# A hybrid decoder step: the first stage in chunk-sized pieces, with logits and two key tiles chunk by chunk

## The chip, the cores and the metric

The kernel runs on one core of one Trainium2 chip. The metric is device time in microseconds (us) from the first to the last instruction of a run with what the runtime adds around it, as the median of several runs. The engines are named as in the profile: PE (TensorE), DVE (VectorE), ACT (ScalarE), POOL (GpSimd) and SP (SyncE, which issues nearly all DMAs here).

## The reference

One trunk layer of a hybrid decoder, for 1024 prompt tokens and 8 sequences of 8 sample tokens (together 1088 columns, d_model 1024):

```python
proj = rmsnorm(h, norm_mix) @ w_in                 # q, k, v, z, b, a, swa q/k/v, merge gates
qkv_c = silu(causal_conv(qkv, conv_buf, conv_w))   # width 4, per channel
q = l2norm(q) * dk**-0.5 ; k = l2norm(k)           # 8 heads of 128
beta = sigmoid(b) ; g = -exp(a_log) * softplus(a + dt_bias)
# gated delta rule in chunks of 64 tokens: cumulative g, decay, a unit lower triangular
# solve of (k*beta) k^T * decay for each chunk and head, then a scan over the chunks
h = h + (sigmoid(gates_a) * o_a + sigmoid(gates_b) * o_b) @ w_out    # o_b: sliding-window attention
h = h + relu(rmsnorm(h, norm_ffn) @ w_up)**2 @ w_down
h = h + sigmoid(rmsnorm(h, norm_ple) @ w_ple_gate) * (p_l @ w_ple_proj)
```

The last factor, `p_l @ w_ple_proj`, depends on nothing else; the kernel computes it first and keeps it in DRAM (`ppd`) until the end.

## The kernel before

Activations stand transposed: 128 features on the partitions, 1088 token columns in the free dimension. The columns are worked in three chunks, `CH`, of 384, 384 and 320. Each fp32 operand of a large product is split into a high part and the rest (`xh`, `xl` for x, `wh`, `wl` for a weight tile), and a product is three matmuls: high by high, low by high, high by low (L166 to L168). One output tile of 128 features is eight k-steps of three matmuls for each of three chunks. A weight tile of 128x1024 is loaded by SP (L119, `wr`, three buffers), split by ACT (L134, `wh`) and POOL (L135, `wl`; the first two on DVE), in the order of the list `order` at L107. Results of PE come in `ps`, three PSUM banks; small ones in `pst`, `psc` (two banks each) and `psn` (one).

The first stage (L274 to L341) does three things side by side:

- p is loaded in three transfers (L284), split on ACT (L286) and DVE (L287), and multiplied into eight output tiles, `ple(f)` (L320). A tile is worked whole: three chunks, evacuated by ACT into one buffer `ppo` of 128x1088 (L328, four buffers), then stored to `ppd` in one DMA of 544 KB (L332).
- x is loaded by chunk in two halves (L294). `x_norm(i)` (L303) squares a chunk on ACT (L306), adds on DVE (L309) and calls `rsqrt_pe` (L238): a matmul with ones (L247, `psn`), scale on DVE (L250), the power -0.5 on POOL (L251), a diagonal `dg` on DVE (L256) and a matmul with it (L257) that lays the factors out along the columns. Then eight times: the scaled x (L316, DVE), `xh` (L317, ACT), `xl` (L318, DVE for two of eight, else POOL).
- The tuple at L335 writes the order of the pieces by hand: `(0, 1, 2, n0, n1, n0, n0, 3, n1, n2, n1, 4, 5, n2, n2, 6, 7)`, a number being one `ple` tile and n0 to n2 the next piece of a chunk's norm.

Each engine then runs its instructions in the order given by a scheduler, which no engine leaves.

After that stage come the logits of the gates (L388, 48 matmuls of 32 rows), their transposes (L427, L430), a chain of some 40 small DVE instructions that makes `beta` and `g` (`gates_tm`, L393 to L422), cumulative sums by matmuls (L435 to L437, L452 to L454), transposes (L465 to L468), and `gcr` stored to DRAM (L469, L473). The key stage follows (L618 to L634): for each of eight heads `conv_steps` (L491) makes one output tile of w_in (order index 8 + h) into `raw` (L500, L502), convolves it (L509 on ACT, L511 three times on DVE, tanh L513, then L522 and L523 into `kT`); `key_rows` (L551) loads the decay row of the head into the one buffer `E` (L556), adds the mask (L558), takes exponents (L564), stores it as `Ed` (L566) and transposes `kT` (L532); `key_products` (L582), one head later, multiplies keys with keys (L591, L592, L593) and stores `kkL` (L596). After heads 3 and 7 the stored products are loaded as `LT` (L601). From there the triangular solve runs on DVE, with L678 and L687 at its head and L666 and L667 as its steps.

## Time and profile of the kernel before

| | |
|---|---|
| Runs (device us) | 2144.75, 2151.54, 2156.72; median 2151.54 |
| The profiled execution | 2145.25 us, its span 2143.5 us |
| Mean granted TensorE clock | 0.989 |
| Busy share | PE 97%, DVE 51%, ACT 37%, POOL 33% |
| Chain that ended last | PE 79%, DVE 10%, ACT 5%, issue 3% |
| DMA | 196.49 MB, mean 92 GB/s |

The profile shows one execution, with all times from the span's start. In the rows further down a line reads: start, duration, engine, line of the kernel, operation, output and inputs, size, count, and in brackets how long the engine was idle just before, with what ended the wait. Matmuls overlap in the rows: what one costs is the distance between two starts. The PEclk of a stretch is the granted clock of TensorE as a share of full speed.

### The profile page before, as it was taken

The numbers are of one execution on the slowest core, as the hardware profiler recorded it, in microseconds if no ns is written. First come the engines' busy times: TensorE is split into PE (matmuls) and PEld (weight loads), VectorE is DVE, ScalarE is ACT, GpSimd is POOL, SyncE is SP. The second block draws the span as 40 slices with busy tenths as digits, with TensorE's granted clock in tenths as the row PEclk, the third lists the DMA queues.
The fourth block names the chain that finished last, engine by engine and source line by source line (L and its number), as shares of the span: only waits on it lengthen the run. The fifth ranks groups of instructions, "written<-read, shape, count | busy, mean of one in ns | idle before, by whom it ended". The sixth has DMA issues, their size and how long they took to land.

```text
span 2143.5 us, 33612 instructions
## 1 busy us (share of the span) xinstructions
PE 2072.6 (97%) x13485; PEld 1994.1 (93%) x13485; DVE 1082.6 (51%) x1717; ACT 798.1 (37%) x1959; POOL 715.1 (33%) x675
## 2 busy tenths in 40 slices
PE   7999999789999999999998999999999999999999
PEld 6899899678889999999998999999999999999998
DVE  6444499787654555455556444233332323333654
ACT  6476434477643443344334223122121212212321
POOL 3332456243235445554456122121212121212121
PEclk9999999899999999999999999999999999999999
DMA  6365343333243223322341221111111111111132
GB/s 238 122 218 182 115 147 109 117 114 119 77 142 103 72 94 121 108 78 71 112 135 64 102 71 44 46 47 43 49 41 50 40 50 40 50 40 50 40 127 80
DMA packets 89063, 196.49 MB, mean 92 GB/s; under 512 B 33612, under 2 KB 44748, under 8 KB 88780
## 3 DMA queue, kind: packets, MB, share of 16 engines
q1 hardware_dynamic: 88908, 194.35, 28.0%
q8 instruction: 106, 1.74, 0.3%
q14 instruction: 49, 0.40, 0.1%
HBM read 145.48 MB, written 50.78 MB: 92 GB/s over the span
## 4 chain that ended last, share of the span: by engine, by line
PE 79%; DVE 10%; ACT 5%; issue 3%; POOL 1%; DMA 1%; SPq 0%; ACTq 0%; DVEq 0%; POOLq 0%
PE ps L166 23%; PE ps L168 22%; PE ps L167 22%; DVE fs L666 2%; DVE LT L667 2%; PE psn L975 1%; PE pst L953 1%; ACT wh L134 1%; DVE nm L938 1%; PE psc L1278 1%; ACT pst L572 1%; ACT pr L940 1%; PE psc L1273 1%; PE pst L1147 1%; PE psc L930 1%
## 5 line engine op out<-in xcount | busy, mean ns | idle before, releaser
L135 POOL TENSOR_TENSOR wl<-wr,wh 128x1024 fp32r<-128x1024 f32 x140 | 342.3, 2445 | 904.6 <-ACT wh L134 904.4
L166 PE MATMUL ps<-xh,wh 128*128 128x384 f32 (+1 forms) x1800 | 624.5, 347 | 3.0 <-ACT qf L350 1.6
L167 PE MATMUL ps<-xl,wh 128*128 128x384 f32 (+1 forms) x1800 | 597.5, 332 | 0.0
L168 PE MATMUL ps<-xh,wl 128*128 128x384 f32 (+1 forms) x1800 | 594.5, 330 | 0.0
L166 PEld LDWEIGHTS ps<-xh,wh 128*128 128x128 f32 x1800 | 341.6, 190 | 14.3 <-issue 9.5
L167 PEld LDWEIGHTS ps<-xl,wh 128*128 128x128 f32 x1800 | 342.3, 190 | 1.3 <-issue 1.1
L134 ACT ACTIVATE wh<-wr 128x1024 fp32r<-128x1024 f32 x143 | 150.8, 1054 | 517.0 <-PE ps L167 441.8
L168 PEld LDWEIGHTS ps<-xh,wl 128*128 128x128 f32 x1800 | 340.6, 189 | 1.6 <-issue 0.7
L166 PE MATMUL ps<-uh,wh 128*128 128x384 f32 (+1 forms) x768 | 250.7, 326 | 1.2 <-DVE h L1429 1.2
L168 PE MATMUL ps<-uh,wl 128*128 128x384 f32 (+1 forms) x768 | 250.9, 327 | 0.0
L167 PE MATMUL ps<-ul,wh 128*128 128x384 f32 (+1 forms) x768 | 250.5, 326 | 0.0
L1429 DVE TENSOR_TENSOR h<-h,ps 128x384 f32<-128x384 f32 (+1 forms) x192 | 100.5, 530 | 226.3 <-PE ps L168 226.3
L166 PE MATMUL ps<-ph,wh 128*128 128x384 f32 (+1 forms) x600 | 196.3, 327 | 0.0
L167 PE MATMUL ps<-pl,wh 128*128 128x384 f32 (+1 forms) x600 | 196.2, 327 | 0.0
L168 PE MATMUL ps<-ph,wl 128*128 128x384 f32 (+1 forms) x600 | 196.0, 327 | 0.0
L1415 DVE TENSOR_TENSOR ul<-us,uh 128x384 fp32r<-128x384 f32 (+1 forms) x96 | 98.0, 1022 | 115.3 <-ACT uh L1414 115.3
L166 PEld LDWEIGHTS ps<-uh,wh 128*128 128x128 f32 x768 | 144.2, 188 | 2.0 <-DVE h L1429 2.0
L168 PEld LDWEIGHTS ps<-uh,wl 128*128 128x128 f32 x768 | 144.2, 188 | 0.0
L167 PEld LDWEIGHTS ps<-ul,wh 128*128 128x128 f32 x768 | 144.1, 188 | 0.0
L511 DVE SCALAR_TENSOR_TENSOR cacc<-raw,cw,cacc 128x1112 f32<-128x1112 f32 x72 | 109.5, 1521 | 59.5 <-ACT cacc L509 58.1
L1413 ACT ACTIVATE us<-ut 128x384 f32<-128x384 f32 (+1 forms) x96 | 48.2, 502 | 196.0 <-DVE ut L1412 194.5
L1412 DVE SCALAR_TENSOR_TENSOR ut<-ps,rb 128x384 f32<-128x384 f32 (+1 forms) x96 | 51.3, 535 | 136.2 <-PE ps L168 136.2
(415 smaller groups left out, 3442.5 us busy)
## 6 DMA issues: line engine op xcount, KB each, us to landing
wr<-win SPq DMA_DIRECT2D x60, 512.0 KB
wr<-wup SPq DMA_DIRECT2D x32, 512.0 KB
wr<-wdn SPq DMA_DIRECT2D x32, 512.0 KB
ppd<-ppo SPq DMA_DIRECT2D x8, 544.0 KB
kTd<-kT SPq DMA_DIRECT2D x8, 544.0 KB
Ed<-E SPq DMA_DIRECT2D x8, 544.0 KB
rg<-Ed SPq DMA_DIRECT2D x8, 544.0 KB
gkT<-kTd SPq DMA_DIRECT2D x8, 544.0 KB
```

The costliest lines, as they stand in the source:

```text
L134: act(hv, rv, AF.Copy)
L135: (nc.gpsimd if i > 1 else nc.vector).tensor_tensor(lv, rv, hv.bitcast(F32), ALU.subtract)
L166: mm(ps[:M, :w], a, h[:, c0 : c0 + w], start=(k == 0), stop=False)
L167: mm(ps[:M, :w], a, l[:, c0 : c0 + w], start=False, stop=False)
L168: mm(ps[:M, :w], b, h[:, c0 : c0 + w], start=False, stop=(k == n - 1))
L511: stt(out=cc, in0=raw[:, j : j + CONVW], scalar=cw[:, f, j : j + 1], in1=cc, op0=ALU.mult, op1=ALU.add)
L666: tt(tmp, X[:, j : j + 1, j + 1 :].broadcast_to(sh), X[:, 0:j, j : j + 1].broadcast_to(sh), ALU.mult)
L667: tt(X[:, 0:j, j + 1 :], X[:, 0:j, j + 1 :], tmp, ALU.add)
L1412: stt(out=t, in0=ps[:, :w], scalar=0.0, in1=rb2[:, c0 : c0 + w], op0=ALU.max, op1=ALU.mult)
L1413: act(s, t, AF.Square)
L1415: tt(lo[:, c0 : c0 + w], s, hi[:, c0 : c0 + w].bitcast(F32), ALU.subtract)
L1429: tt(hc, hc, ps[:, :w], ALU.add)
```

## The change

The order of the first stage is written out anew, in pieces of one chunk:

- The four steps of a projection tile go chunk by chunk: `ple(fs, i)` does the tiles of the list fs for chunk i alone, each into a buffer `ppo` of 128x384 (13 buffers, shared with the pieces of p). Their stores (`spill`) are 24 of 192 or 160 KB instead of 8 of 544 KB, and come later.
- p is loaded in six transfers instead of three, half of x chunk 0 before p chunk 1, the constants before x chunks 1 and 2.
- The squares stand in two half buffers; `rsqrt_steps` yields once more, between the power and the diagonal.
- The narrow weight `wba` (for the logits) moves behind the first key tile in the order of weights, with split buffers of its own.
- The logits and the first two key tiles (order index 8 and 9) are no longer done after all of x is ready, but chunk by chunk between the norms. Their raw results have buffers of their own. Everything that follows them (gate chain, both convolutions) starts when the third chunk of each is done.

```diff
-    order = [(d["wpp"][u], 1024) for u in range(2)] + [(d["wba"], 128)]
+    order = [(d["wpp"][u], 1024) for u in range(2)]
     order += [(d["win"][f], 1024) for f in WIN_ORDER]
+    order.insert(3, (d["wba"], 128))
...
-        for step in (0, 1, 2, n0, n1, n0, n0, 3, n1, n2, n1, 4, 5, n2, n2, 6, 7):
-            if isinstance(step, int):
-                ple(step)
-            else:
-                next(step, None)
...
+    p_chunk(0)
+    w_load()
+    w_split()
+    x_chunk(0, 0)
+    p_chunk(1)
+    x_chunk(0, 4)
+    p_chunk(2)
+    w_load()
+    w_split()
+    load_constants()
...
+    def spill(fs, i):
+        c0, w = CH[i]
+        for f in fs:
+            dma(ppd[f, :, c0 : c0 + w], ppo[f, i][:, :w])
...
+    A, B1, B2 = range(4), range(4, 6), range(6, 8)
+    ple(A, 0)
+    ple(A, 1)
+    next(n0)
+    spill(A, 0)
+    ple(A, 2)
+    next(n0)
+    ple(B1, 0)
+    next(n0)
+    next(n0, None)
+    next(n1)
+    spill(A, 1)
+    spill(A, 2)
+    ple(B1, 1)
+    ple(B1, 2)
+    next(n1)
+    ple(B2, 0)
+    next(n1)
+    next(n1, None)
+    next(n2)
+    ple(B2, 1)
+    ple(B2, 2)
+    dma(cache, d["cachec"])
...
+    first = [conv_steps(8 + h, lambda: kp, key_tile, ep.tile([P, RAWW], F32, name="raw0", tag="tg")) for h in range(2)]
+    logits = logit_steps()
+    next(first[0])
+    next(logits)
+    next(first[1])
+    next(n2)
+    next(n2)
+    next(n2, None)
+    for st in (first[0], logits, first[1]):
+        next(st)
+    for i in range(3):
+        spill(B1, i)
+        spill(B2, i)
+    for st in (logits, *first):
+        next(st)
...
     for h in range(H + 2):
-        st = conv_steps(8 + h, kp, key_tile) if h < H else feature_steps()
-        next(st)
-        if h > 1:
+        if h < 2:
+            st = first[h]
+        else:
+            st = conv_steps(8 + h, kp, key_tile) if h < H else feature_steps()
+            next(st)
             key_products(*todo.pop(0))
-        next(st)
-        next(st)
+            next(st)
+            next(st)
```

The scheduler's order on ACT, in the middle of the first stage, before: `ppo` is the evacuation of a projection bank, `xh` the high part of a scaled column group.

```order
L306 ACTIVATE xsq<-xc_155 128x4x320
L317 ACTIVATE xh<-xc_139 128x384 x2
L306 ACTIVATE xsq<-xc_155 128x4x320
L317 ACTIVATE xh<-xc_139 128x384 x4
L134 ACTIVATE wh<-wr 128x8x16
L317 ACTIVATE xh<-xc_139 128x384
L328 ACTIVATE ppo<-ps 128x384 x2
L317 ACTIVATE xh<-xc_139 128x384
L328 ACTIVATE ppo<-ps 128x320
```

And now, at the same place:

```order
L404 ACTIVATE ppo<-ps 128x384 x3
L384 ACTIVATE xh<-xc_126 128x384
L404 ACTIVATE ppo<-ps 128x384
L384 ACTIVATE xh<-xc_126 128x384 x2
L404 ACTIVATE ppo<-ps 128x320
L137 ACTIVATE wh<-wr 128x1024
L384 ACTIVATE xh<-xc_126 128x384 x4
L404 ACTIVATE ppo<-ps 128x320
L384 ACTIVATE xh<-xc_126 128x384
```

Banks were emptied only after seven `xh`; now evacuations stand between them, but the last one of this place still stands behind the split of a whole weight tile and four `xh`.

On PE before, the gates' products stood in the first key tile (`ps<-xl,wh` and the like), 35 products after its start:

```order
L166 MATMUL ps<-xh,wh 128x384
L435 MATMUL pst<-g,cst 128x64
L436 MATMUL pst<-g,cst 128x64
L437 MATMUL pst<-g,cst 128x64
L452 MATMUL pst<-gs,c_82 64x8
L453 MATMUL pst<-gs,c_82 64x8
L167 MATMUL ps<-xl,wh 128x384
L454 MATMUL pst<-gbs,cst 128x64
L168 MATMUL ps<-xh,wl 128x384
```

And now they stand in the fourth key tile, four products after its start, and the first head's key products (L664, the L591 of before) come ahead of them:

```order
L171 MATMUL ps<-xh,wl 128x384
L664 MATMUL psc<-kT 128x128 x8
L169 MATMUL ps<-xh,wh 128x320
...
L169 MATMUL ps<-xh,wh 128x384
L543 MATMUL pst<-g,cst 128x64
L544 MATMUL pst<-g,cst 128x64
L545 MATMUL pst<-g,cst 128x64
L560 MATMUL pst<-gs,c_82 64x8
L561 MATMUL pst<-gs,c_82 64x8
```

The gates moved from the first key tile to three tiles later, behind a product that needs the first head's finished `kT`.

On DVE before, the gate chain was over when the first convolution came:

```order
L422 SCALAR_TENSOR_TENSOR gs<-lg,ea 64x8
L450 TENSOR_TENSOR gbs<-gs,c_82 64x64
...
L653 TENSOR_TENSOR dec_2461<-dec_2461,msk_2462 64x64
L511 SCALAR_TENSOR_TENSOR cacc<-raw,cw,cacc 128x1112 x2
L558 TENSOR_TENSOR E<-E,cst 128x1024
L511 SCALAR_TENSOR_TENSOR cacc<-raw,cw,cacc 128x1112
L560 TENSOR_TENSOR E<-E,c_82 64x64
L522 SCALAR_TENSOR_TENSOR kT<-raw,cacc 128x1024
```

And now two convolutions (`raw_520` and `raw_521`, lines L315 and L326) stand within the gate chain:

```order
L315 SCALAR_TENSOR_TENSOR cacc<-raw_520,cw,cacc 128x1112
L522 TENSOR_TENSOR lg_864<-lg_864 128x64
L522 TENSOR_TENSOR lg_893<-lg_893 64x8
L315 SCALAR_TENSOR_TENSOR cacc<-raw_521,cw,cacc 128x1112
L523 TENSOR_SCALAR lg_864<-lg_864 128x64
L523 TENSOR_SCALAR lg_893<-lg_893 64x8
L326 SCALAR_TENSOR_TENSOR kT<-raw_520,cacc 128x1024
...
L528 SCALAR_TENSOR_TENSOR lg<-lg_893,lg 64x8
L326 SCALAR_TENSOR_TENSOR kT<-raw_521,cacc 128x1024
L530 SCALAR_TENSOR_TENSOR g<-lg,ea 128x64
```

Before, no convolution stood ahead of `g`; now two whole ones do.

Farther on DVE, the decay row of head 4 (`E<-E,cst`) before, between the convolutions of the last two key tiles:

```order
L511 SCALAR_TENSOR_TENSOR cacc<-raw,cw,cacc 128x1112 x3
L558 TENSOR_TENSOR E<-E,cst 128x1024
L560 TENSOR_TENSOR E<-E,c_82 64x64
L522 SCALAR_TENSOR_TENSOR kT<-raw,cacc 128x1024
L523 SCALAR_TENSOR_TENSOR kT<-raw,cacc 128x64
L592 TENSOR_TENSOR kk<-psc,E 128x512 x2
L511 SCALAR_TENSOR_TENSOR cacc<-raw,cw,cacc 128x1112 x3
```

And now:

```order
L315 SCALAR_TENSOR_TENSOR cacc<-raw,cw,cacc 128x1112 x3
L631 TENSOR_TENSOR E<-E,cst 128x1024
L633 TENSOR_TENSOR E<-E,c_82 64x64
L665 TENSOR_TENSOR kk<-psc,E 128x512 x2
L326 SCALAR_TENSOR_TENSOR kT<-raw,cacc 128x1024
L327 SCALAR_TENSOR_TENSOR kT<-raw,cacc 128x64
L631 TENSOR_TENSOR E<-E,cst 128x1024
```

The convolution ahead of head 4's decay row is now that of the last key tile, and none follows: four heads' rows come behind it one after the other. From the 1122nd row of PE before (the 1128th now) the two programs have the same rows on every engine.

## Rows read from the trace of the kernel before

**Rows 1.** The page: busy time by engine, and the chain that ended last by engine.

```profile
PE 2072.6 (97%) x13485; PEld 1994.1 (93%) x13485; DVE 1082.6 (51%) x1717; ACT 798.1 (37%) x1959; POOL 715.1 (33%) x675
PE 79%; DVE 10%; ACT 5%; issue 3%; POOL 1%; DMA 1%; SPq 0%; ACTq 0%; DVEq 0%; POOLq 0%
```

**Rows 2.** PE, the instructions that ended a wait in the first 100 us; with 69.45 and 73.65 the heads of two groups of the gates' products, with 70.65 and 74.51 the product of the key tile that follows each; 93.39 is the first matmul of the third key tile.

```profile
12.43 0.96 PE L166 MATMUL ps<-phi,wh 128*128 128x320 f32 x2 [1.22 <-ACT phi L286]
33.45 0.69 PE L166 MATMUL ps<-phi,wh 128*128 128x384 f32 x1 [3.33 <-ACT ppo L328]
48.22 0.68 PE L257 MATMUL pst<-dg,cst 128*128 128x128 f32 x4 [3.07 <-DVE dg L256]
69.45 0.41 PE L435 MATMUL pst<-g,cst 128*128 128x64 f32 x2 [1.66 <-DVE lg L420]
70.65 0.69 PE L167 MATMUL ps<-xl,wh 128*128 128x384 f32 x1
73.65 0.41 PE L465 MATMUL pst<-cst,gc 128*64 128x128 f32 x1
74.51 0.69 PE L167 MATMUL ps<-xl,wh 128*128 128x384 f32 x1
93.39 0.42 PE L166 MATMUL ps<-xh,wh 128*128 128x384 f32 x1
```

**Rows 3.** Stretches of the first stage and, last, one of the key stage: the stretch, its length, then busy time (and count) of PE, PEld, DVE, ACT and POOL, the granted clock, the DMA share and GB/s.

```profile
33.40:39.60 6.20, 6.10 (x20) 5.81 (x21) 6.20 (x8) 2.50 (x6) 5.26 (x5) 0.50 0.50 174
39.60:48.20 8.60, 5.55 (x35) 5.21 (x34) 6.35 (x12) 5.08 (x12) 7.35 (x8) 1.00 0.59 206
48.20:53.40 5.20, 5.17 (x22) 4.19 (x23) 4.16 (x11) 2.72 (x6) 1.71 (x2) 0.67 0.01 2
60.60:69.40 8.80, 7.19 (x44) 6.50 (x43) 7.34 (x43) 2.89 (x9) 3.32 (x9) 1.00 0.29 101
69.40:77.20 7.80, 7.75 (x30) 6.49 (x31) 1.57 (x9) 2.25 (x13) 0.00 (x0) 0.56 0.02 4
197.70:204.00 6.30, 6.09 (x44) 5.44 (x45) 0.04 (x1) 5.90 (x24) 1.81 (x2) 1.00 0.93 280
```

**Rows 4.** SP's issues of the first four projection stores.

```profile
18.96 6.54 SPq L332 DMA_DIRECT2D ppd<-ppo  x4
```

**Rows 5.** DVE: beginning, two members and end of the gate chain; one step of the first convolution and the `kT` that ends it.

```profile
62.02 0.29 DVE L401 COPY lg<-pst 128x64 f32<-128x64 f32 x2 [5.44 <-PE pst L430]
62.82 1.83 DVE L406 TENSOR_SCALAR beta<-beta 128x64 f32<-128x64 f32 x1
64.99 0.15 DVE L406 TENSOR_SCALAR betas<-betas 64x8 f32<-64x8 f32 x1
69.60 0.22 DVE L450 TENSOR_TENSOR gbs<-gs,c 64x64 f32<-64x64 f32 x1
87.99 1.37 DVE L511 SCALAR_TENSOR_TENSOR cacc<-raw,cw,cacc 128x1112 f32<-128x1112 f32 x1
90.73 1.22 DVE L522 SCALAR_TENSOR_TENSOR kT<-raw,cacc 128x1024 f32<-128x1024 f32 x1 [1.25 <-ACT raw L513]
```

**Rows 6.** ACT, tanh and first factor of a convolution; POOL, the weight split that ran beside the gate chain.

```profile
89.58 1.11 ACT L513 ACTIVATE raw<-cacc 128x1112 f32<-128x1112 f32 x1
97.20 1.22 ACT L509 ACTIVATE cacc<-raw,cw 128x1112 f32<-128x1112 f32 x1
62.21 2.39 POOL L135 TENSOR_TENSOR wl<-wr,wh 128x1024 fp32r<-128x1024 f32 x1 [0.83 <-ACT wh L134]
```

**Rows 7.** SP, one turn of the decay buffer: head 5's row stored, head 6's loaded.

```profile
197.28 0.33 SPq L566 DMA_DIRECT2D Ed<-E  x1
...
200.32 0.33 SPq L556 DMA_DIRECT2D E<-gcd  x1
```

**Rows 8.** DVE, the decay buffer in the later heads: mask and first product of head 4, the convolution of the last key tile, mask (ended by the landing of the row) and first product of head 6, first product of head 7.

```profile
175.86 1.22 DVE L558 TENSOR_TENSOR E<-E,cst 128x1024 f32<-128x1024 f32 x1
178.50 0.68 DVE L592 TENSOR_TENSOR kk<-psc,E 128x512 f32<-128x512 f32 x1
187.68 5.71 DVE L511 SCALAR_TENSOR_TENSOR cacc<-raw,cw,cacc 128x1112 f32<-128x1112 f32 x3 [7.38 <-ACT cacc L509]
205.04 2.82 DVE L558 TENSOR_TENSOR E<-E,cst 128x1024 f32<-128x1024 f32 x1 [7.30 <-DMA E<-gcd]
209.45 0.69 DVE L592 TENSOR_TENSOR kk<-psc,E 128x512 f32<-128x512 f32 x1 [1.46 <-ACT E L564]
225.14 0.69 DVE L592 TENSOR_TENSOR kk<-psc,E 128x512 f32<-128x512 f32 x1 [1.26 <-ACT E L564]
```

**Rows 9.** The key products on PE: those of heads 0 and 1 from the chain of waits, those of head 6 from the timeline.

```profile
98.25 1.78 PE psc L591 x16
113.39 1.78 PE psc L591 x16
...
197.71 2.18 PE L591 MATMUL psc<-kT 128*128 128x128 f32 x16 [1.66 <-ACT kb L593]
```

**Rows 10.** The head of the solve: SP's load of the last four heads' products, and DVE's first instructions of the solve.

```profile
230.05 0.79 SPq L601 DMA_DIRECT2D LT<-kkL  x2
241.61 0.80 DVE L678 TENSOR_TENSOR bsol<-bsol,rk 128x64 f32<-128x64 f32 x1 [14.61 <-ACT rk L677]
242.71 5.46 DVE L687 TENSOR_TENSOR LT<-LT,br 128x1024 f32<-128x1024 f32 x4
```

More of the change, by code (lines that the diff above doesn't have):

```diff
@@ L112, in hybrid_layer @@
     order += [(d["wpg"][f], 1024) for f in range(KT)]
-    wst = dict(raw=[], split=[], used=0)
+    wst = dict(raw=[], split=[], used=0, narrow=None)
     def w_load():
@@ L263, in col_rsqrt_pe @@
         for c0, w in CH:
-            rsqrt_pe(acc[:, c0 : c0 + w], c0, w, mul, add, rb, np_)
+            for _ in rsqrt_steps(acc[:, c0 : c0 + w], c0, w, mul, add, rb, np_):
+                pass
     def squares(src, np_):
@@ new lines, in hybrid_layer, with ple @@
+    wpl, ppo = [None, None], {}
+    def ple(fs, i):
+        c0, w = CH[i]
+        for f in fs:
+            if f % 4 == 0 and i == 0:
+                wpl[:] = next_w()
+            ppo[f, i] = pp.tile([P, 384], F32, name="ppo", tag="ppo", bufs=13)
+            ps = pg.tile([P, 512], F32, name="ps", tag="ps")
+            for k in range(2):
+                o = k * 512 + f % 4 * P
+                wh, wl = (z[:, o : o + P] for z in wpl)
+                h_, l_ = (z[:, c0 : c0 + w] for z in prhs[k])
+                mm(ps[:, :w], wh, h_, start=(k == 0), stop=False)
+                mm(ps[:, :w], wh, l_, start=False, stop=False)
+                mm(ps[:, :w], wl, h_, start=False, stop=(k == 1))
+            act(ppo[f, i][:, :w], ps[:, :w], AF.Copy, scale=0.5)
@@ new lines, in spill @@
+    def spill(fs, i):
+        c0, w = CH[i]
+        for f in fs:
+            dma(ppd[f, :, c0 : c0 + w], ppo[f, i][:, :w])
+    A, B1, B2 = range(4), range(4, 6), range(6, 8)
+    n0, n1, n2 = (x_norm(i) for i in range(3))
+    ple(A, 0)
[16 more added lines that the diff above has]
+    next(n1, None)
@@ new lines, in hybrid_layer, with logit_steps, key_tile @@
+    next(n2)
+    ple(B2, 1)
+    ple(B2, 2)
+    dma(cache, d["cachec"])
+    def logit_steps():
+        wb, _ = next_w()
+        for c0, w in CH:
+            ps = pg.tile([P, 512], F32, name="ps", tag="ps")
+            for k in range(KT):
+                for i in range(2):
+                    mm(ps[:32, :w], wb[:, k * 32 : k * 32 + 32], xs[k][i][:, c0 : c0 + w], start=(k + i == 0), stop=(k + i == KT))
+            act(ba[:, c0 : c0 + w], ps[:32, :w], AF.Copy)
+            yield
+    def key_tile():
+        kT = kp.tile([P, NP + MS], F32, name="kT", tag="kT")
+        nc.gpsimd.memset(kT[:, T:], 0.0)
+        return kT
```

198 lines of the change are left out of this document (89 added, 109 removed).

## The prediction

> **What bounds the kernel now.** I read the page first: PE is busy 97% of the span and carries 79% of the chain that ended last [rows 1]. Nothing here removes a matmul, so a gain can come only from time in which PE waits or runs at a lower clock. Such time lies in the first 94 us. The waits of PE there [rows 2] are 1.22 us for the third piece of p, 3.33 us for a bank that ACT empties late, 3.07 us for the diagonal of chunk 2, and 1.66 us for the gates. The stretches show more [rows 3]: 3.05 us idle between 39.6 and 48.2 (8.60 less 5.55), 1.61 us between 60.6 and 69.4, and after each long wait a granted clock of 0.50, 0.67 and 0.56, the 1.2 GHz level for most of those stretches. What the change is worth is therefore how much earlier the third key tile, at 93.39 [rows 2], can begin, less what is given back before the next thing that sets the end, the start of the solve on DVE at 242.71 [rows 10]. From there the programs are the same, row for row.
>
> **The change, part by part: what it saves.** Seven terms, each as the time by which the third key tile comes earlier.
>
> - Projection chunk by chunk. Four tiles of chunk 0, then of chunk 1, need p's last piece some eight groups later than before. The 1.22 us at 12.43 go: **1.2 us**.
> - The bank wait at 33.45. Evacuations are now spread between the `xh`, but the last bank stands behind a weight split and four more `xh`. I keep the wait and the slow stretch behind it (6.20 us at 0.50): **0**. If both went, it would be 3.33 and half of 6.20, together 6.4 us; that is the upper bound.
> - The wait for chunk 2. PE now has two pieces of key tiles of 24 products and a piece of the logits of 16 to do while chunk 2's factors are made; of 3.05 us idle I keep half: **1.5 us** (bounds 0 and 3.05).
> - The slow stretch behind that wait: 5.20 us at 0.67 would be 3.5 us at full clock: **1.7 us**.
> - The idle 1.61 us between 60.6 and 69.4, gate wait included, leave this place: **1.6 us**.
> - The stretch 69.4 to 77.2, 7.80 us at 0.56, becomes 4.4 us: **3.4 us**.
> - The gates' own products leave: 69.45 to 70.65 and 73.65 to 74.51, 2.06 us at the low clock, so about 1.0 us of the 4.4, and I add 1.0 us for the logits' transposes, which run in the stretch from 60.6: **2.0 us**.
>
> The sum is 1.2 + 1.5 + 1.7 + 1.6 + 3.4 + 2.0 = **11.4 us**; the third key tile starts near 82 instead of 93.4.
>
> Three edits cost nothing. The weight list's new order: the split that it moves runs on ACT and POOL while PE has a piece of the projection to do; the cover gone, it is one 2.39 us of POOL [rows 6]. The half-size squares: the same elements on ACT and DVE. The constants before x chunks 1 and 2: chunk 1's factors are not reached before POOL has finished the `xl` of chunk 0.
>
> The stores are 24 instead of 8, the loads of p six instead of three. The first four issues of 544 KB took 6.54 us on SP, waits included [rows 4]; 16 more stores at a few tenths of a microsecond each are some 6 us of SP, spread over 60 us in which SP feeds no load that PE waits for. I price them at 0; the bound, if a weight load queues behind a whole group of them, is 6.54 us once.
> The Trainium skill, "DMA: Bandwidth & Descriptors", section "Bandwidth", advises batches of at least 1 MiB for 75% of the peak, which speaks against cutting 544 KB into 192 and 160 KB. By it the bound of 6.5 us and not 0 would stand in the sum, and the front would gain 4.9 instead of 11.4 us. The trace agrees only in part: from 33.4 us on, where most of the stores now lie, the first stage moves 2 to 206 GB/s [rows 3], which leaves room for slower transfers.
>
> **What it gives back.** Both convolutions and the gate chain now begin together, when the third chunk of tiles 8 and 9 is evacuated, around 78 to 80 us. A convolution on DVE is three steps of 1.37 us and 1.22 us for `kT` (with the sample columns 1.4), with tanh on ACT (1.11) and the first factor (1.22) [rows 5, 6]; 5.6 us of DVE each. The gate chain ran from 62.02 to 69.82, 7.8 us [rows 5]. DVE has thus 19 us to do from about 79.7, all in front of `g`, which is ready near 98.5.
>
> - PE reaches head 0's key products 48 products into tile 10, about 8.3 us after its start, at 90. `kT` needs four of the convolution steps, about half of the gates and one tanh: 79.7 + 5.5 + 3.9 + 1.1 + 1.4 = 91.6, with the ACT hand-overs near 92. Wait: **2.1 us** (bounds 0, and 5.6 if both convolutions are finished first).
> - PE reaches the gates 28 products farther, near 97.2, and waits to 98.5: **1.3 us** (bounds 0 and 3.4, the gates' wait with a stretch at the low clock).
> - The gates' products and transposes are done here at full clock: **2.0 us**.
>
> Do these waits bring the low clock again? The gates' 1.66 us did, after a stretch in which PE was busy 7.19 of 8.80 us; the 1.66 us at 197.71 did not (clock 1.00) [rows 3, 9]. What precedes now is a stretch without idle time, which is nearer to 197.71, so 0; the bound is 3.4 us.
>
> What remains at head 1 is 11.4 - 2.1 - 1.3 - 2.0 = **6.0 us**. Head by head PE then takes 15.14 us (98.25 to 113.39 [rows 9]) as before.
>
> **The start of the solve.** It needs `rk` (ACT, before 241.61) and the loaded products, issued at 230.05 [rows 10]. The first comes from PE and is 6 us earlier. The second hangs on one buffer, E. Head 4's row now stands on DVE behind the convolution of the last key tile: 187.68 less 6.0, plus 5.71, is 187.4, against 175.86 before [rows 8]. From there heads 4 to 7 follow each other through the one buffer. One turn before: store at 197.28, load at 200.32, mask at 205.04, first product at 209.45 [rows 7, 8]; 12.2 us, or 10.6 if the mask takes 1.22 and not 2.82; with two products of 0.69 ahead of the store 12.0 to 13.6. The last turn took 15.7 (209.45 to 225.14), with other work of DVE in it. Head 7's first product thus comes between 187.4 + 2.6 + 3 x 12.0 = 226.0 and 187.4 + 2.6 + 13.6 + 2 x 15.7 = 235.0, against 225.14. I take 228.5, in the lower half, since only the last turn held such other work; the load is then issued 3.4 us later, at 233.4. A row of 512 KB took 4.7 us from issue to the mask, and this load is twice that size, so it lands 4.7 to 9.4 us after: 238.1 to 242.8. The solve starts there, and not at 242.71 less 6.0. I take the lower end, as both halves are issued at once: 242.7 - 238.1 = 4.6, and **4 us** in round terms is what is left. It is reckoned against the profiled execution: 2145.25 - 4 = 2141.3. That run lies 6.3 us under the median of 2151.54; runs scatter by 12 us. From the middle of the two, 2148.4, I forecast **2144 us**. About 0.5%, 10.7 us, is what a measurement can tell from no change.
>
> **The rivals.**
>
> *The gain is kept, or more* (0.28). The waits at head 0's products and at the gates don't occur since ACT and DVE overlap better, and the bank wait shrinks: 11.4 - 2.0 = 9.4 up to 15.8 us with the 6.4 of the bank. For it: DVE was busy only 1.57 of the 7.80 us from 69.4 [rows 3], so that work put there is cheap. Against it: the order stands, `kT` behind gates and convolution. Time 2132.6 to 2139.
>
> *The gain is swallowed* (0.15): the DVE backlog is longer, and clock and waits come back at the new place. Price 3.4 for the clock, and the difference in the gates: the `beta` of 128x64 took 1.83 us while a weight split of 2.39 us ran on POOL from 62.21, its 64x8 sister 0.15 [rows 5, 6]; three such splits fall into the backlog, each up to 1.7 us more, 5 in all. 4 less 3.4 less up to 5 is -4.4 to +0.6: time 2148 to 2153.
> The Trainium skill, "SBUF — State Buffer", section "Who interferes with whom", states the rule for that: VectorE and GpSimd share a pair of ports under an exclusive lock, and the loser blocks for a whole instruction. By that rule each split costs DVE an instruction's length, the 1.83 us agree with it, and the time would be the upper of the two.
>
> *Slower: the one decay buffer sets the solve* (0.15). The change keeps all gains in front, but head 4 waits for the last tile's convolution. Its point: a solve later than 242.71 needs head 7's first product after 228.4 if the load takes 9.4 us, after 233.1 if it takes 4.7. At 235.0 the load is issued at 239.9 and lands at 244.6 to 249.3, so the solve starts 1.9 to 6.6 us later than before: 2150 to 2155. For it: the convolution ahead of head 4's row is one tile later. Against it: the turn before was bound by other DVE work at the last head.
>
> **How the numbers follow.** Forecast 0.42 (its own range 2140 to 2148), kept 0.28, swallowed 0.15, decay buffer 0.15. Range 2128 to 2156: the kept gain's 2132.6 with most of the runs' half scatter of 6 us below it, and the upper end of the slower cases with 1 us. Faster by over 10.7 us: most of the kept case and a little of the forecast, 0.30. Slower by over 10.7 us: the ends of the two slower cases, 0.07. Within: 0.63.
>
> **What will show it.** Third key tile's first matmul near 82; no wait of 1.2 us at p; the bank wait still there near 33; waits of 2.1 and 1.3 us near 92 and 98; the solve's first use of the products near 239, its releaser the load rather than `rk`. A first tile not earlier than 88, or a solve after 243, makes the prediction wrong.

## The result and the profile after

The changed kernel is **slower**: 2158.13 us as the median of 20 runs, against 2147.23 us for the kernel before (20 runs); the ratio is 1.0045 with a 95% interval of 1.003 to 1.006, some 10 us. The forecast was 2144 us and its range ended at 2156. The profiled execution took 2160.55 us, with a span of 2158.8 us.

The front went nearly as forecast. The stretches of the first stage after, which answer to [rows 3], with the same columns:

```profile
28.00:33.40 5.40, 1.58 (x9) 1.00 (x7) 5.40 (x9) 4.92 (x11) 5.06 (x5) 1.00 0.94 317
33.40:39.60 6.20, 2.68 (x10) 2.31 (x11) 5.18 (x3) 2.45 (x5) 6.20 (x4) 0.51 0.26 87
39.60:48.20 8.60, 8.60 (x44) 8.60 (x45) 5.65 (x11) 4.57 (x9) 1.80 (x5) 0.76 0.71 223
60.60:69.40 8.80, 8.45 (x49) 6.74 (x48) 5.82 (x13) 4.18 (x10) 5.97 (x8) 1.00 0.00 0
69.40:77.20 7.80, 7.80 (x51) 7.17 (x50) 0.00 (x0) 1.32 (x4) 2.28 (x10) 1.00 0.01 2
```

The stretch from 69.4 ran at full clock with 51 matmuls in place of 30 at 0.56. The waits of PE after, from the timeline, with the starts of key tiles among them, each the first product at 128x384 (L169). The third key tile, which is number 10 in the order of weights, starts at 83.31 and answers to 93.39 in [rows 2]; tiles 13, 14 and 15 start at 131.77, 149.26 and 171.71:

```profile
8.01 0.69 PE L401 MATMUL ps<-phi,wh 128*128 128x384 f32 x1 [8.01 <-ACT wh L137]
...
32.20 0.41 PE L401 MATMUL ps<-phi,wh 128*128 128x320 f32 x1 [3.77 <-ACT ppo L404]
...
38.80 1.41 PE L250 MATMUL psn<-cst,xsq 128*128 128x1 f32 x6 [3.51 <-DVE xsq L377]
...
83.31 0.45 PE L169 MATMUL ps<-xh,wh 128*128 128x384 f32 x1
...
93.48 2.05 PE L664 MATMUL psc<-kT 128*128 128x128 f32 x16 [1.57 <-DVE kT L326]
...
131.77 0.34 PE L169 MATMUL ps<-xh,wh 128*128 128x384 f32 x1
...
134.29 2.19 PE L664 MATMUL psc<-kT 128*128 128x128 f32 x16 [1.64 <-ACT kb L666]
...
149.26 0.34 PE L169 MATMUL ps<-xh,wh 128*128 128x384 f32 x1
...
152.11 3.10 PE L664 MATMUL psc<-kT 128*128 128x128 f32 x16 [2.34 <-ACT kb L666]
...
169.77 2.18 PE L664 MATMUL psc<-kT 128*128 128x128 f32 x16 [1.31 <-ACT kb L666]
...
171.71 0.42 PE L169 MATMUL ps<-xh,wh 128*128 128x384 f32 x1
...
236.88 0.69 PE L169 MATMUL ps<-xh,wh 128*128 128x384 f32 x1 [5.34 <-ACT qf L290]
...
242.38 0.48 PE L213 MATMUL psc<-nhi,sel 128*2 128x384 f32 x1 [4.17 <-ACT nhi L222]
```

Tile 10 starts 10.1 us earlier than before, and tile 13 7.1 us (131.77; 138.83 in the timeline of before). Tile 14 is 4.7 us ahead (153.99 before), tile 15 2.6 us behind (169.14 before). Then come waits of 5.34 and 4.17 us; with one of 0.28 us behind them they make 9.8 us, where the kernel before had 3.2 at this place (231.77 to 234.67 in its timeline). The key products of all eight heads, grouped, show the same (durations in ns: least, median, greatest; then the starts of the first and the last); first the changed kernel, then the one before:

```profile
L664 PE MATMUL psc<-kT x128: 271/276/516, 93.5 to 226.1; 128*128 128x128 f32 x128
```

```profile
L591 PE MATMUL psc<-kT x128: 270/275/377, 98.1 to 214.1; 128*128 128x128 f32 x128
```

4.6 us earlier with the first head, 12.0 us later with the last: the lead is lost, and more, between them.

On DVE the decay rows and the head of the solve, which answer to [rows 8] and [rows 10]:

```profile
112.48 1.23 DVE L631 TENSOR_TENSOR E<-E,cst 128x1024 f32<-128x1024 f32 x1 [0.54 <-DMA E<-gcd]
129.55 1.22 DVE L631 TENSOR_TENSOR E<-E,cst 128x1024 f32<-128x1024 f32 x1
147.38 1.22 DVE L631 TENSOR_TENSOR E<-E,cst 128x1024 f32<-128x1024 f32 x1
159.50 5.62 DVE L315 SCALAR_TENSOR_TENSOR cacc<-raw,cw,cacc 128x1112 f32<-128x1112 f32 x3 [7.36 <-ACT cacc L313]
165.03 1.22 DVE L631 TENSOR_TENSOR E<-E,cst 128x1024 f32<-128x1024 f32 x1
167.94 0.69 DVE L665 TENSOR_TENSOR kk<-psc,E 128x512 f32<-128x512 f32 x1 [0.17 <-ACT E L637]
...
192.93 1.22 DVE L631 TENSOR_TENSOR E<-E,cst 128x1024 f32<-128x1024 f32 x1
...
204.36 1.23 DVE L631 TENSOR_TENSOR E<-E,cst 128x1024 f32<-128x1024 f32 x1 [0.92 <-DMA E<-gcd]
...
217.22 1.23 DVE L631 TENSOR_TENSOR E<-E,cst 128x1024 f32<-128x1024 f32 x1 [7.54 <-DMA E<-gcd]
...
231.44 1.21 DVE L631 TENSOR_TENSOR E<-E,cst 128x1024 f32<-128x1024 f32 x1
234.04 0.69 DVE L665 TENSOR_TENSOR kk<-psc,E 128x512 f32<-128x512 f32 x1 [1.26 <-ACT E L637]
251.37 0.81 DVE L748 TENSOR_TENSOR bsol<-bsol,rk 128x64 f32<-128x64 f32 x1 [15.47 <-ACT rk L747]
252.48 1.23 DVE L757 TENSOR_TENSOR LT<-LT,br 128x1024 f32<-128x1024 f32 x1
```

Head 0's mask (112.48) stood at 86.85 before. From it on, mask follows mask in 17.1, 17.8 and 17.7 us, where PE alone took 15.14 [rows 9]. The turn can be read between head 2 and head 3. SP's issues there:

```profile
151.68 0.32 SPq L639 DMA_DIRECT2D Ed<-E  x1
154.51 0.33 SPq L629 DMA_DIRECT2D E<-gcd  x1
```

Store at 151.68, load at 154.51, and with the 4.7 us that a row took [rows 7, 8] the row is there near 159.2 by estimate, 5.8 us ahead of its mask at 165.03. On DVE the three convolution steps from 159.50 stand between, and these had waited 7.36 us for ACT, not for the row. The transfers thus don't set this turn. It closes over the orders of ACT and DVE, which the turn before shows without a gap:

```profile
131.16 2.44 ACT L637 ACTIVATE E<-E,ngc 128x128 f32<-128x128 f32 x8
...
139.70 1.23 ACT L313 ACTIVATE cacc<-raw,cw 128x1112 f32<-128x1112 f32 x1
...
148.99 2.43 ACT L637 ACTIVATE E<-E,ngc 128x128 f32<-128x128 f32 x8
```

```profile
141.05 6.41 DVE L315 SCALAR_TENSOR_TENSOR cacc<-raw,cw,cacc 128x1112 f32<-128x1112 f32 x3 [6.73 <-POOL E L634]
```

On ACT the exponents of head 1 (131.16) stand ahead of the first factor of the next convolution (139.70), and from the start of the one to the end of the other ACT works 9.8 us without idling. On DVE that convolution takes 6.4 us and stands ahead of the mask of head 2 (147.38). On ACT a tanh and an evacuation, 1.5 us, stand ahead of head 2's exponents (148.99). Together these are the 17.8 us. (The trace names an instruction of POOL as the convolution's releaser; it ended at 140.98, the first factor at 140.93.) From the start of the first factor to the start of the exponents it is 8.9, 9.3 and 8.5 us for heads 1 to 3, since a whole convolution stands between. In the kernel before it was 1.1, 1.7 and 3.9 us, since there the mask stood ahead of the convolution or behind its first step. Head 2's turn then, on ACT:

```profile
127.48 1.23 ACT L509 ACTIVATE cacc<-raw,cw 128x1112 f32<-128x1112 f32 x1
...
129.13 2.46 ACT L564 ACTIVATE E<-E,ngc 128x128 f32<-128x128 f32 x8
```

With these shorter ways the turn of 17.8 us would by estimate have been 10 to 13, under PE's 15.14, so that PE set the pace. And where a mask of the changed kernel did wait for its row (heads 5 and 6, at 204.36 and 217.22, released by the DMA), it came 11.4 and 12.9 us after the mask before it: the chain of the buffer by itself is shorter than PE's turn.

PE, which needs the banks of the products, gets to start head by head at 134.29, 152.11 and 169.77, 17.8 and 17.7 us apart, after waits of 1.64, 2.34 and 1.31 us. The longest of these was followed by a lower clock (granted clock, the third column from the end):

```profile
149.26:152.11 2.85, 0.51 (x4) 0.19 (x2) 2.20 (x4) 2.80 (x11) 0.25 (x2) 1.00 0.01 3
152.11:160.00 7.89, 7.89 (x46) 7.74 (x47) 0.53 (x2) 6.69 (x25) 3.68 (x7) 0.78 0.89 301
```

At 0.78 a part of these 7.89 us ran at 1.2 GHz; at full clock the same work would by estimate have taken 0.78 x 7.89 = 6.2 us, so 1.7 us are the clock's, beside the 2.34 of the wait.

At the end the solve starts at 252.48, 9.8 us later than before. That is nearly the whole difference of the medians, 10.9 us. The two profiled spans differ by 15.3 us; the rest lies between 410 and 710 us and goes with the mean granted clock (0.984 here, 0.989 before), which differs as much among runs of one kernel: 0.988 went with 2152.6 us, 0.979 with 2169.1 us. The experiments below are therefore read by the ratio of their runs and by the start of the solve.

### The profile page after: what moved, and what is told of

The parts are those of the page before. It is cut to its first block, busy times and chain, and to the rows that moved or that the text cites. A ratio compares the mean times of both kernels' runs of the same rounds, so it can differ in the third digit from the quotient of the medians.

```text
span 2158.8 us, 33650 instructions
## 1 busy us (share of the span) xinstructions
PE 2077.5 (96%) x13485; PEld 1998.9 (93%) x13485; DVE 1091.6 (51%) x1720; ACT 799.8 (37%) x1962; POOL 715.8 (33%) x675
## 4 chain that ended last, share of the span: by engine, by line
PE 73%; DVE 9%; ACT 3%; issue 2%; POOL 1%; SPq 0%; DMA 0%; ACTq 0%; DVEq 0%; POOLq 0%
PE ps L169 21%; PE ps L171 21%; PE ps L170 21%; DVE fs L736 2%; DVE LT L737 2%; PE psn L1045 1%; PE pst L1023 1%; DVE nm L1008 1%; PE psc L1348 1%; ACT wh L137 1%; PE psc L1343 1%; PE pst L1217 1%; PE psn L1360 1%; PE psc L1000 1%; DVE pr L1004 1%
## 5 line engine op out<-in xcount | busy, mean ns | idle before, releaser
L169 PE MATMUL ps<-xh,wh 128*128 128x384 f32 (+1 forms) x1800 | 627.3, 348 | 6.8 <-ACT qf L290 5.3
L169 PEld LDWEIGHTS ps<-xh,wh 128*128 128x128 f32 x1800 | 343.3, 191 | 18.2 <-issue 9.3
L169 PE MATMUL ps<-uh,wh 128*128 128x384 f32 (+1 forms) x768 | 251.2, 327 | 1.2 <-DVE h L1499 1.2
L169 PE MATMUL ps<-ph,wh 128*128 128x384 f32 (+1 forms) x600 | 196.8, 328 | 0.0
L315 DVE SCALAR_TENSOR_TENSOR cacc<-raw,cw,cacc 128x1112 f32<-128x1112 f32 x72 | 115.3, 1601 | 65.8 <-ACT cacc L313 50.9
L169 PEld LDWEIGHTS ps<-uh,wh 128*128 128x128 f32 x768 | 144.3, 188 | 2.0 <-DVE h L1499 2.0
```

Source lines behind the costliest of these rows:

```text
L169: mm(ps[:M, :w], a, h[:, c0 : c0 + w], start=(k == 0), stop=False)
L315: stt(out=cc, in0=raw[:, j : j + CONVW], scalar=cw[:, f, j : j + 1], in1=cc, op0=ALU.mult, op1=ALU.add)
```

## The experiments

Theory A: late gates make the decay rows late, and the one decay buffer then sets a turn longer than PE's. Theory B: the late stores and small loads collide with the key stage's transfers. Theory C: two convolutions at once on DVE. D and E split A: what makes the turn long is the mask's place behind the convolution in DVE's order (D; the trace above adds the exponents' place on ACT), or the buffer's own chain of transfers (E).

| run | ratio to before, 95% | start of the solve, us |
|---|---|---|
| kernel before | 1 | 242.7 |
| changed kernel | 1.0045 [1.003, 1.006] | 252.5 |
| 1 gates first | 1.0032 [1.0014, 1.0051] | 252.9 |
| 2 two decay buffers | 0.9963 [0.9946, 0.998] | 238.4 |
| 3 before, late gates | 1.0049 [1.0026, 1.0071] | 251.9 |
| 4 before, two buffers | 0.999 [0.9972, 1.0008] | 235.6 |
| 5 mask on POOL | 1.0132 [1.011, 1.0154] | 271.7 |
| 6 before, mask on POOL | 1.0035 [1.0017, 1.0053] | 252.5 |
| 7 gates first, two buffers | 1.0 [0.9981, 1.0018] | 239.7 |
| 8 two buffers, tiles late | 1.0005 [0.9984, 1.0025] | 243.8 |
| 9 gates first, pinned | 1.0035 [1.0011, 1.0059] | 252.4 |
| 10 pinned | 1.0018 [0.9998, 1.0039] | 252.8 |
| 11 store untied | 1.0034 [1.0012, 1.0056] | 246.4 |
| 12 before, pinned | 1.0027 [1.0008, 1.0046] | 248.6 |
| 13 before, late gates, two buffers | 1.0014 [0.9997, 1.0031] | 241.7 |
| 14 gates first, part pinned | 1.0016 [1.0, 1.0032] | 247.5 |
| 15 gates first, pinned to 12 | 1.0003 [0.9982, 1.0023] | 246.8 |

The start of the solve is read from one execution of each kernel. It goes with the ratio in most rows, but not in all: run 4 starts it 7.1 us earlier than the kernel before and is 0.1% faster, run 10 starts it 10.1 us later and is 0.2% slower.

**1. Gates first.** Edit: the gate chain's code ahead of the third chunks of the early tiles.

```diff
-    for st in (logits, *first):
-        next(st)
+    next(logits)
     pctx.close()
...
+    for st in first:
+        next(st)
     def conv_tile(f, cvp, dst):
```

> The changed kernel, but the gate chain stands in the code right after the logits' third chunk and ahead of the third chunks of the two early key tiles. Theory A (late gates): in the changed kernel g was ready at 99.4 us instead of 69.1, head 0's decay row was masked at 112.5 instead of 86.9, and from there the one decay buffer set a turn of 17.6 us per head where PE needs 15.1; with g near 80 the heads run at 15.1 again, the early start of the third key tile (83.3 against 93.4) is kept in part, and the time falls 10 to 16 us below the changed kernel, to 2142 to 2148, which is 0 to 6 us under the kernel before. Theory B (the 24 late stores and six p loads collide with the key stage's transfers): gates make no difference, within 2 us of the changed kernel. Theory C (two convolutions at once on DVE): they are still behind the gates, so at most the 1.6 us of PE's wait for kT come back.

Measured 1.0032: theory A's number failed. On DVE `g` (L529) came 15 us earlier and the first mask (L633) 8.6 us earlier, but the turn grew to 18.5 us, with a convolution (L315) and the `kT` that ends it (L326) ahead of each mask:

```profile
84.55 0.22 DVE L529 SCALAR_TENSOR_TENSOR g<-lg,ea 128x64 f32<-128x64 f32 x1
103.83 1.22 DVE L633 TENSOR_TENSOR E<-E,cst 128x1024 f32<-128x1024 f32 x1
113.70 6.22 DVE L315 SCALAR_TENSOR_TENSOR cacc<-raw,cw,cacc 128x1112 f32<-128x1112 f32 x3 [5.44 <-ACT cacc L313]
121.20 1.23 DVE L326 SCALAR_TENSOR_TENSOR kT<-raw,cacc 128x1024 f32<-128x1024 f32 x1 [1.28 <-ACT raw L317]
122.34 1.22 DVE L633 TENSOR_TENSOR E<-E,cst 128x1024 f32<-128x1024 f32 x1
140.84 1.22 DVE L633 TENSOR_TENSOR E<-E,cst 128x1024 f32<-128x1024 f32 x1
```

The turn closes as in the changed kernel, with `kT` added: on ACT the exponents of head 0 start at 105.08 and the first factor ends at 113.58, on DVE the convolution ends at 119.92, `kT` waits for the tanh, then the mask, and head 1's exponents start at 123.59. The edit also gives up most of what the front had won: the third key tile starts at 90.00, not 83.31. Theory B's number (no difference) fits this run too; run 2 speaks against it.

**2. Two decay buffers.** Edit, with a small tile shared to make room:

```diff
-        E = kp.tile([P, T], F32, name="E", tag="E", bufs=1)
+        E = kp.tile([P, T], F32, name="E", tag="E", bufs=2)
...
-    kks = sv.tile([NS, H * NS], F32, name="kks")
+    kkt = sv.tile([P, H * NS], F32, name="kks")
+    kks = kkt[:NS]
...
-        kb = kp.tile([P, 8, 64], F32, name="kb", tag="kb", bufs=1)
+        kb = kkt.rearrange("p (c f) -> p c f", f=64)
```

> The changed kernel with two decay buffers instead of one; to make room, the small tile for the keys' second product shares a buffer with another half-used tile. Theory A: a row's load and mask no longer wait for the store of the row before, which is 7 us of a turn of 12 to 17.6; head 7's first product moves from 234.0 toward 222 to 228 and the time falls 5 to 10 us, to 2148 to 2153. If the turn closes over the banks of the key products or over the order on DVE instead of over the buffer, under 3 us. Theory B: within 2 us of the changed kernel. Theory C: within 2 us.

Measured 0.9963, more than expected: the solve starts 14.1 us earlier than in the changed kernel, and the kernel is faster than the one before by 0.2 to 0.5%. The gates are as late and the stores as many as in the changed kernel. With run 4, where a second buffer wins next to nothing, theories B and C fall as causes of the loss. On DVE the mask of head 1 now stands ahead of the next convolution:

```profile
115.12 1.22 DVE L632 TENSOR_TENSOR E<-E,cst 128x1024 f32<-128x1024 f32 x1 [1.44 <-DMA E<-gcd]
...
126.15 6.07 DVE L315 SCALAR_TENSOR_TENSOR cacc<-raw,cw,cacc 128x1112 f32<-128x1112 f32 x3 [2.83 <-ACT cacc L313]
```

On ACT the exponents of head 2 start at 136.60, 1.1 us behind the start of a first factor (135.48). The second buffer thus changed the orders as well as the transfers. The run shows that the loss comes with the one buffer; it doesn't part the two.

**3. The kernel before with late gates.** Edit: the first two tiles' chunks, then (at the line of dots) the gate chain's code as it was, then the loop.

```diff
+    first = [conv_steps(8 + h, kp, key_tile) for h in range(2)]
+    for st in first:
+        for _ in range(3):
+            next(st)
...
     todo = []
     for h in range(H + 2):
-        st = conv_steps(8 + h, kp, key_tile) if h < H else feature_steps()
+        st = first[h] if h < 2 else conv_steps(8 + h, kp, key_tile) if h < H else feature_steps()
```

> The kernel before, with nothing of the new first stage, but the gate chain stands in the code behind the three chunks of the first two key tiles, as in the changed kernel. Theory A: g comes some 25 us later than before and head 0's decay row too; the one buffer sets 17.6 us per head from the first head, so the solve starts 10 to 20 us later and the time is 2157 to 2167. Theory B: no stores moved, so within 3 us of the kernel before. Theory C: the two convolutions meet the gates on DVE as in the changed kernel, a wait of 1 to 3 us, so 2148 to 2151.

Measured 1.0049, as theory A said: late gates alone, with the old first stage, cost as much as the whole change. `g` came at 98.35, the masks of heads 0 to 3 at 112.20, 129.95, 148.03 and 164.34, within 0.8 us of the changed kernel's. The third key tile started at 85.94: of the 10.1 us by which the changed kernel brings it forward, 7.5 come from moving the gates out of its way.

**4. The kernel before with two buffers.** Edit: `bufs=2` as in 2, without the shared tile.

> The kernel before with two decay buffers. If the decay buffer bounds the solve only in the changed kernel, this gains 0 to 3 us, since its turn sets only heads 4 to 7 and PE had 15.1 us per head up to head 3 (2144 to 2147). If it bounds the kernel before as much, 5 to 10 us (2137 to 2142), and what two buffers win in the changed kernel says nothing on the change.

Measured 0.999, within the first expectation in time; the solve started 7.1 us earlier, more than the 3 us allowed for. So the old kernel too was held by the buffer in its last heads, but two buffers win 0.82% in the changed kernel (0.9963 over 1.0045) and 0.1% here.

**5 and 6. The mask on POOL.** Edit in both kernels:

```diff
-        tt(E[:, :NP].rearrange("p (c n) -> p c n", n=P), ..., ALU.add)
-        tt(E[:NS, NP:T], E[:NS, NP:T], maskqs, ALU.add)
+        nc.gpsimd.tensor_tensor(E[:, :NP].rearrange("p (c n) -> p c n", n=P), ..., ALU.add)
+        nc.gpsimd.tensor_tensor(E[:NS, NP:T], E[:NS, NP:T], maskqs, ALU.add)
```

> The changed kernel, one decay buffer, with the mask added to the decay row on POOL instead of DVE. The run with the gates first showed g at 84.6 and still 18.5 us from mask to mask, so the late gates alone don't set the turn. Theory D (place in DVE's order): the mask stands behind the three steps of the next tile's convolution, which are themselves behind PE and the banks of the key products; off DVE the turn loses 5 to 6 us and PE's 15.1 us per head set the pace again; head 7's first product before 226 (234.0 in the changed kernel), time 2141 to 2148. Theory E (the buffer's own chain of store, load, mask, exponents): store to load 2.9, landing 4.7, mask 2.4 on POOL with a weight split of 2.4 at times ahead, exponents 2.4, products 1.9 make 14.3 to 16.7 us, so half of it stays: 2150 to 2154.

> The kernel before with the mask on POOL. Theory D: there the mask stood ahead of the convolution or within it for heads 0 to 3 and only heads 4 to 7 were behind one, so 0 to 6 us faster than before (as with two buffers: about 2 us). Theory E: no difference or up to 3 us slower, since POOL is the slower engine.

Both gains that theory D predicted failed: 1.0132 and 1.0035, and theory E's numbers failed with them, since both kernels are slower than it allowed. The timeline of POOL and DVE in run 5:

```profile
110.77 2.40 POOL L631 TENSOR_TENSOR E<-E,cst 128x1024 f32<-128x1024 f32 x1
125.49 3.15 POOL L631 TENSOR_TENSOR E<-E,cst 128x1024 f32<-128x1024 f32 x1
```

```profile
123.02 8.20 DVE L315 SCALAR_TENSOR_TENSOR cacc<-raw,cw,cacc 128x1112 f32<-128x1112 f32 x3 [6.64 <-ACT cacc L313]
134.10 0.69 DVE L665 TENSOR_TENSOR kk<-psc,E 128x512 f32<-128x512 f32 x1 [0.24 <-issue]
```

The mask no longer waits for the convolution, but the products (L665) still stand behind it on DVE, and on ACT the exponents stand behind its tanh: they start at 132.74, though the mask was over at 128.64, and 19.5 us after those of head 0 (113.21). The convolution takes 8.20 us beside a POOL that works first on a weight split (from 122.81) and then on the mask; in run 1 it took 6.22 beside a weight split alone. What stands behind the convolution was not the mask alone, and theory D's remedy was wrong. By the time alone the run doesn't tell D from E; in the trace it is again an order, here ACT's, that holds the turn.

**7. Gates first and two buffers.** Edits 1 and 2 together.

> The changed kernel with both edits, the gates ahead of the third chunks of the early tiles and two decay buffers. If the late gates cost anything once the decay buffer is out of the way, 2 to 6 us less than with two buffers alone (ratio 0.9963): about 0.994 of the kernel before. If they don't, the same within 2 us.

Measured 1.0: not better than two buffers alone, rather 0.4% worse. Putting the gates first wins nothing once there are two buffers. That late gates then cost nothing isn't shown: the edit also moves the start of the third key tile from 83.43 in run 2 to 90.28, and run 13 speaks against it.

**8. Two buffers, early tiles given up.** Edit: in the kernel of run 2, all of `n2` first, then three chunks each of tile 8, logits and tile 9.

> The changed kernel with two decay buffers, but the logits and the two first key tiles come whole after all of x is ready, as before; only the projection, the loads of p and the late stores remain of the new first stage. If the early tiles make the 10 us by which the third key tile came earlier, this is 6 to 10 us slower than with them (ratio 0.9963), so within 0.2% of the kernel before with two buffers (0.999) or above it. If the projection by chunks makes them, within 3 us of 0.9963.

Measured 1.0005, 0.4% above run 2, in the direction and of the size of the first expectation: the early tiles are worth that much in time. They don't make the 10 us at the third key tile, though: it started at 85.75, against 83.43 in run 2 and 85.94 in run 3, which has the old first stage. The rest of the 0.4% arises behind it, and how isn't shown.

**9, 10 and 12. The convolution pinned behind the mask.** Edit in three kernels (gates first; changed; before): the scheduler keeps these steps behind all that stands ahead of them in the code on DVE.

```diff
-            stt(out=cc, in0=raw[:, j : j + CONVW], ...)
+            i = stt(out=cc, in0=raw[:, j : j + CONVW], ...)
+            if 10 <= f < 16:
+                tc.keep_in_program_order(i)
```

> The changed kernel with the gates first and one decay buffer, and the convolution steps of tiles 10 to 15 pinned on DVE in the order of the code, that is behind the mask of the head before. With the gates first alone, the turn stayed 18.5 us: the row landed near 115.3 while DVE was in the convolution from 113.7 to 119.9, and the mask came at 122.3. Theory D: with the mask in front of the convolution the turn is store to load 2.9, landing 4.7, mask 1.2, exponents 1.5, products 1.9, about 12 to 13 us, under PE's 15.1, so PE sets the pace, the solve starts 8 to 14 us earlier than with the gates first alone (252.9) and the time is 2140 to 2147, ratio 0.996 to 0.999. Theory E (the buffer's chain alone is longer than 15.1): within 3 us of the gates first alone (ratio 1.0032).

> The changed kernel, gates late as they are, one buffer, with the same pins. Theory D: the pace becomes PE's, but tile 10's convolution now waits once for head 1's mask near 124 instead of running at 104, so PE waits some 9 us for that tile's kT and the lead of the first stage is spent: 2150 to 2156, 2 to 8 us below the changed kernel. If the late gates did no harm of their own, as fast as with gates first and pins (2140 to 2147). Theory E: 2158 or above.

> The kernel before with the pins, as a control: heads 0 to 3 keep their order, heads 4 to 7 get the mask ahead of the convolution. 0 to 6 us faster (about as with two buffers, 0.999); if pins cost or win something by themselves it shows here.

Run 9 missed (1.0035), though the mask of head 1 came at 115.25, ahead of the convolution, where run 1 had it at 122.34. From PE's timeline tile 10 started at 89.93 and tile 11 17.7 us later; from there to tile 15 the starts were 14.8 to 15.7 us apart, PE's pace. But behind the last pinned tiles a new wait came, on PE and DVE; the row for which DVE waits was issued only at 162.37, on SP behind the store of a `kT` (161.91):

```profile
189.43 1.97 PE L609 MATMUL pst<-cst,kT 128*128 128x128 f32 x8 [8.91 <-DVE kT L328]
```

```profile
171.03 2.17 DVE L635 TENSOR_TENSOR E<-E,cst 128x1024 f32<-128x1024 f32 x1 [9.81 <-DMA E<-gcsd]
```

Run 10 came out at 1.0018, inside the 2150 to 2156 us that theory D gave, though its interval overlaps with the changed kernel's, with waits of PE for `kT` that sum to 15.0 us in place of those for the banks. Run 12 is 0.3% slower than the kernel before, not faster: pins cost something by themselves.

**11. The store untied.** Edit: `dma(Ed[h], E)` becomes `dma(Ed[h], kT[:, :T])`.

> The changed kernel with the store of the decay row taken from the kT of the same head instead of E (same size, so later stages read wrong rows): the transfers stay, but E's next load no longer waits for the store. The 2.9 us between store and load leave the turn: 17.7 becomes 14.8 and PE's 15.1 set the pace (theories D and E both): 2147 to 2153. If the load then lands before the convolution begins and the scheduler's order still puts the convolution first, the turn is set by PE, convolution, mask, products and banks without any transfer, and nothing is won (within 3 us of 2158).

In time it is the second expectation (1.0034, median 2158.27 us), with an interval of 1.0012 to 1.0056 that reaches into the first. The solve started 6.1 us earlier than in the changed kernel; the first turns were 17.1, 16.1 and 17.3 us, not 14.8. Most of the turn is not the store.

**13. Late gates, two buffers, old first stage.** Edits 3 and 4 together.

> The kernel before with late gates (as in the third experiment, ratio 1.0049, start of the solve 251.9) and two decay buffers, nothing of the new first stage. If the late gates cost only through the turn of the one buffer, two buffers take all of it back: solve at 236 to 245, ratio 0.997 to 1.002. If late gates cost something else too, the ratio stays above 1.003.

Measured 1.0014, solve at 241.7: two buffers take the start of the solve back from 251.9 to 241.7, inside what theory A said. Not all of it is taken back, though: against run 4, which differs by the gates alone, the solve starts 6.1 us later, and the ratio is 0.2% higher, with intervals that just overlap. By the start of the solve, late gates cost something else too.

**14 and 15. Gates first, only tiles 10 to 13, or 10 to 12, pinned.**

> The changed kernel with gates first, one buffer, and only tiles 10 to 13 pinned behind the mask, so that the last two tiles, whose pins brought a wait of 8.9 us for kT, are free again. Theory D: heads 1 to 3 run at PE's pace as with all pins (tile starts 14.8 to 15.3 us apart), the 8.9 us don't come, the solve starts near 242 to 246 and the ratio is 0.997 to 1.001. If the order on DVE is not what keeps the turn long, the solve stays near 252 and the ratio near 1.003.

> As the run before with tiles 10 to 12 pinned. The same two expectations; it tells whether the loss moves with the last pinned tile (one long gap between tile starts right behind it) or goes.

Measured 1.0016 and 1.0003, the solve at 247.5 and 246.8: 1.5 and 0.8 us beyond theory D's range for the solve, near or inside its range for the ratio, and 5 to 6 us earlier than with the gates first and no pins (252.9). The 8.9 us are gone. In run 14 the mask of head 1 waits for its row, with DVE idle, and comes 11.6 us after head 0's (104.44):

```profile
116.04 2.88 DVE L635 TENSOR_TENSOR E<-E,cst 128x1024 f32<-128x1024 f32 x1 [7.17 <-DMA E<-gcd]
```

Tile 15 started at 169.21 and 169.65, in run 1 at 176.88. With the mask ahead of the convolution in the first heads, half of the loss in the start of the solve goes, with one buffer. The intervals of the ratios overlap with run 1's.

## Why the prediction was wrong

- **The front was right.** The third key tile was forecast near 82 and started at 83.31. Of the 11.4 us of the sum 7.0 were the gates' (1.6 + 3.4 + 2.0) and 4.4 all else; run 3, with the gates moved and nothing more, gained 7.5, and the changed kernel 10.1, so 2.6 are left for all else. The wait for p went, the bank wait stayed (3.77 us), the idle times and slow stretches of 60 to 77 us went. Two sizes were off: the first matmul came 1.3 us later (8.01), and PE waited 3.51 us at 38.80 for the sums of chunk 1, which now stand behind chunk 0's scaling on DVE; the forecast had the wait for chunk 2 there (it fell to 0.34 us).
- **The give-back was right in size.** 1.57 us at the first products (2.1 forecast), 0.66 us at the gates (at 103.20; 1.3 forecast). From 93.48 to 100 PE ran at full clock, as forecast. At tile 13 7.1 us were left where 6.0 were forecast for the time behind the gates.
- **The step that failed** is that "Head by head PE then takes 15.14 us" as before. From head 2 to head 4 the products are 17.8 and 17.7 us apart. The forecast began the decay buffer's turns only at head 4, from an order row, and let heads 0 to 3 follow PE. But head 0's row came 25.6 us later than before, behind the late gates (`g` at 99.4, against 69.1), and for heads 1 to 3 each mask stood behind a whole convolution in DVE's order, and the exponents in ACT's behind that convolution's first factor and tanh. In place of PE's 15.14 us the turn was the sum of what stands in these two orders, 17.8 us; the lead fell from 7.1 us at tile 13 to -2.6 at tile 15. Runs 2, 3 and 13 show that the loss comes with the one decay buffer and that late gates are enough to bring it about; run 1, that they are not the only way to it: with `g` early again the turn was as long, in the same orders. Runs 14 and 15 show that the mask's place is a part of it. The buffer's own chain, where it was the limit in the changed kernel and in run 14, took 11.4 to 12.9 us.
- **The rival of the decay buffer named the right buffer and the wrong route.** It was given 0.15 and 1.9 to 6.6 us; the solve came 9.8 us later. Head 7's first product came at 234.04, within the forecast's 226 to 235 and near the rival's 235.0, but the rival had the buffer bind from head 4 on only. It was to delay the load of the products; in fact the solve waited 15.47 us for `rk`, which comes from PE. ACT served head 7's exponents (232.73 to 235.18) before the evacuation `qf` at 236.34, for which PE had waited 5.34 us; then 4.17 us for `nhi`, behind an ACT instruction (`nsq`, at 241.01) whose own wait of 4.19 us the trace puts down to nothing it shows. In run 1 it names a releaser for the same instruction: the store of head 7's decay row, `Ed<-E`. In the changed kernel that store was issued at 236.08, and in run 11, where no store reads E, the instruction didn't wait. So it was probably this store, and the late buffer reached the solve through it too. So "`rk` comes from PE and is 6 us earlier" failed as well. In run 2, with two buffers, neither wait is there.
- **Swallowed gain.** The low clock did come back, at 152.11, but by 1.7 us, behind a wait that the buffer's turn makes and not where the forecast feared it. The beta of 128x64 took 1.84 us again, as forecast for one such split.
- **What stays open:** why the scheduler makes these orders with one buffer; how much of what a second buffer wins is the order and how much the transfers; what late gates cost beside it (run 13 against run 4); and whether head 7's store released ACT at 241.01.

The best kernel of the study is the changed one with two decay buffers: 0.9963 [0.9946, 0.998] of the kernel before.

## What to carry to other kernels

A stage that is moved forward drags behind it whatever feeds the next stage from the old place: trace each of the new order's inputs to their producer. Then price the turn of every single-buffered tile against the pace of the engine that bounds, in two ways: the buffer's own chain (store, load, landing), and the loop through the in-order engines, that is all that stands in their orders between an instruction and the same instruction of the next turn. A row that has landed helps nothing if its first user stands behind other work. Where the longer of the two exceeds the pace, a lead shrinks turn by turn, and a gain at the front can become a loss a few turns on. If two kernels differ by about as much as their runs scatter, read the start of a late stage in the trace beside the median, as a help and not in its place.
